# A hybrid encoder layer on one core: weights rounded earlier, weight sums pipelined, and work tied behind other work

## The chip, the core and the metric

The kernel runs on one core of a Trainium2 chip. Its engines run side by side and synchronise through semaphores: PE multiplies matrices, DVE works elementwise with two inputs, ACT evaluates functions, copies and casts, POOL does slow elementwise work, and SP only issues DMAs. The metric is the device time of one execution in microseconds (us), and the median of several runs is compared. The text calls on-chip memory SBUF, the accumulator banks PSUM, and the DRAM behind the chip DRAM.

## The reference

One layer on x of 1024 tokens by 1024 features, everything in float32:

```python
h = rmsnorm(x, g1)
p = h @ w_in                               # gb, gc, gv | q, k, v, go | two low-rank gates
y_a = gb * dwconv3(gc * gv)                # short convolution over tokens, 512 columns
y_b = silu(go) * headnorm(gla(q, k, v) + flipped gla)   # 4 heads of gated linear attention
x = x + rmsnorm(concat(y_a, y_b) @ w_out, gpost)
h = rmsnorm(x, g2)
u = dwconv3(h @ w_up)                      # 5632 columns: 2816 gate, 2816 value
x = x + rmsnorm((silu(u_gate) * u_value) @ w_down, gpost2)
```

## The kernel before

Every float32 product is made of three PE passes. An operand is split by `split` (L671) into a rounded high part (an ACT cast) and a rest (a DVE subtraction); high times high, high times low and low times high are added in PSUM. So nearly every PE operand needs one ACT and one DVE instruction after its DMA has landed.

**Mixer.** Per-token norms and transposes give hT; the value columns come first (tile `pv`, L328). The small low-rank gate values `lr` (L336 to L338) are transposed by PE as `plr` (L397). `swish_gate` (L598) makes one tile of silu(go) for each of four heads (PE tile `pgo`). Attention (`gla_head`, L451) then alternates with the convolution columns (`conv_tile`, L604): states S, outputs `po`, their norm `on` (L585, L589), the transposes `pot` (L595), and the convolution's `u`. Attention's work tiles have tags of their own (qd, kd, m, cum, kin, koT, sq, cc, cu, S).

**Output projection.** `w_out` is loaded in eight row tiles (wo4 to wo7, then wo0 to wo3) through a ring of three raw tiles and split into `woh` and `wol` (L676 to L684). The y tiles are split into yh and yl (L687), and `w_out_tile` (L699) multiplies them (tile `pw`, L709).

**Up stage.** The up product and the down product use a Strassen-type scheme of seven products on 2x2 blocks (Winograd's form), so sums of weight blocks are needed beside the weights. POOL makes them in units: `up_begin` and `up_end` (24 units wu0 to wu23), `down_begin` and `down_end` (11 units wd0/1 to wd20/21). A unit loads two tiles, does four elementwise operations and stores the result to DRAM. `side` (L135) runs the next unit. It is called eight times in the mixer; in the up stage `up` (L937) calls it with a tiny ACT copy `pace` (L959), which each of a unit's loads waits for; the remainder runs at L1078. `up(c)` runs over 22 column tiles c; its PSUM banks pa, pb, pc are added by DVE into `cv` and `cg` (L956, L975, L978, L986, L989). `gate_and_store` (L1000) convolves both (uv, uu), applies SiLU (L1006) and multiplies (L1008); products and their sums go to DRAM as `actd`.

**Down stage.** Seven products in the order 2, 1, 3, 6, 5, 7, 4 over eleven pairs q. `operands` (L1037) loads an activation half (`actd`) and a weight half (w_down or the stored sums `wdd`), and splits them; `big_product` (L1066) multiplies (tiles pda to pdd, L1063). `evict` (L1081) takes banks out with ACT or DVE. At the end each row tile is squared, scaled (yg, L1128 and L1134), added to the saved x2 (`x2r`, L1113) and stored (L1123); rows 0 to 3 are complete before the last product, rows 4 to 7 finish with it.

**What sets the order.** The program is written in Python order, and a scheduler places each engine's instructions; an engine executes its own list strictly in order. `keep` pins instructions, tile rings bound how early a load can start, and all DMAs but POOL's are issued by SP in order.

Of the kernel before, what the change touches and what calls it, by code (L numbers as in the profile page):

```python
# [40 lines left out]
def kernel(
# [50 lines left out]
    def up_begin(i, tile, after):  # L92
# [163 lines left out]
    lrT = gp.tile([96, L], F32R, tag="lrT", name="lrT")  # L256

# [3 lines left out]
    with ExitStack() as n1:  # L261
# [111 lines left out]
        for t in range(1, NT):  # L373
# [12 lines left out]
            if t >= 2:  # L386
                side(after=hs[t][:, 0:1])
# [52 lines left out]
    mp = mix.enter_context(tc.tile_pool(name="mp", bufs=1))  # L440
# [4 lines left out]
    yT = [None] * KT  # L445
# [3 lines left out]
    nc.vector.memset(S[DK:P, NC - 1, :], 0.0)  # L449

    def gla_head(h):  # L451
# [46 lines left out]
        A = mp.tile([P, HALF], F32, tag="A", name=f"A{h}")  # L498
# [21 lines left out]
        def states(i):  # L520
# [14 lines left out]
            for par in range(2):  # L535
# [6 lines left out]
                nc.scalar.copy(S[DK:P, c0 - 1 : c0 - 1 + 2 * n - 1 : 2, :], kvv[DK:P, par, i0:4, :])  # L542
# [122 lines left out]
    act2 = ffn.enter_context(tc.tile_pool(name="act2", bufs=3))  # L665
# [27 lines left out]
    cvp = ffn.enter_context(tc.tile_pool(name="cvp", bufs=3))  # L693
# [87 lines left out]

    n_raw = [0]
# [216 lines left out]

    def gate_and_store(c, cg, cv):  # L1000
# [21 lines left out]
        nc.sync.dma_start(out=act_d[q][:, 3:5, :], in_=z12)  # L1022
        nc.sync.dma_start(out=act_d[q][:, 5:7, :], in_=z34)
# [13 lines left out]
    def operands(m, q, tile=None):  # L1037
# [3 lines left out]
        nc.sync.dma_start(out=raw[:, 0, :], in_=act_d[q][:, w[0], :])  # L1041
# [13 lines left out]
        split(h, l, raw)  # L1055
# [22 lines left out]
    while jobs:  # L1078
        side()
    y += [row_tile(f"y{t}") for t in range(4, NT)]  # L1080
    def evict(rows, half, bank, add=None):  # L1081
        for t in range(4):
# [3 lines left out]
            else:  # L1086
                nc.vector.tensor_add(o, y[add[0] + t][:, add[1]], bank[t])
# [98 lines left out]
```

## Time and profile before

| | us |
|---|---|
| median of three runs | 1088.48 (1084.95 to 1091.08) |
| the profiled execution's own time | 1082.93 |
| its span, first to last instruction | 1081.2 |
| PE busy | 1056.0 |
| DVE, ACT, POOL busy | 794.9, 466.2, 343.4 |

The granted clock is 0.997 of full speed over the span. A matmul row's duration overlaps the next one's, so a stretch's pace is read from the starts. A timeline row gives the start, the duration, the engine, the line, the operation and tiles; a bracket gives the idle time just before it and what ended that idle time.

### The profile page before, as it was taken

The numbers are of one execution on the slowest core, as the hardware profiler recorded it, in microseconds if no ns is written. First come the engines' busy times: TensorE is split into PE (matmuls) and PEld (weight loads), VectorE is DVE, ScalarE is ACT, GpSimd is POOL, SyncE is SP. The second block draws the span as 40 slices with busy tenths as digits, with TensorE's granted clock in tenths as the row PEclk, the third lists the DMA queues.
The fourth block names the chain that finished last, engine by engine and source line by source line (L and its number), as shares of the span: only waits on it lengthen the run. The fifth ranks groups of instructions, "written<-read, shape, count | busy, mean of one in ns | idle before, by whom it ended". The sixth has DMA issues, their size and how long they took to land.

```text
span 1081.2 us, 14384 instructions
## 1 busy us (share of the span) xinstructions
PE 1056.0 (98%) x5409; PEld 871.2 (81%) x5409; DVE 794.9 (74%) x990; ACT 466.2 (43%) x654; POOL 343.4 (32%) x358
## 2 busy tenths in 40 slices
PE   8999999999999999999999999999999999999997
PEld 7988887788887888777888888888888788878876
DVE  6641369879837657989987987987798867645685
ACT  6422354453326335544444434344444435334651
POOL 2785200000000000045465554547456455440000
PEclk9999999999999999999999999999999999999999
DMA  8776211110106423168877867775877789977783
GB/s 281 270 257 208 85 40 37 41 40 21 39 21 233 156 79 108 60 189 271 290 230 259 275 230 243 252 261 153 256 254 273 281 290 322 329 274 229 263 261 152
DMA packets 163800, 211.17 MB, mean 195 GB/s; under 512 B 18305, under 2 KB 113682, under 8 KB 163730
## 3 DMA queue, kind: packets, MB, share of 16 engines
q1 hardware_dynamic: 144594, 141.04, 40.6%
q0 software_dynamic: 19136, 69.21, 18.3%
q8 instruction: 42, 0.69, 0.3%
q14 instruction: 28, 0.23, 0.1%
HBM read 147.04 MB, written 63.18 MB: 194 GB/s over the span
## 4 chain that ended last, share of the span: by engine, by line
PE 33%; DMA 20%; POOL 20%; issue 12%; DVE 11%; ACT 3%; SPq 0%; DVEq 0%; POOLq 0%; ACTq 0%
PE pw L709 7%; PE pgc L223 4%; PE pgo L223 4%; PE pv L328 4%; PE pgv L223 3%; PE pqk L223 3%; PE pgb L223 2%; PE pdb L1063 2%; DVE d L673 2%; DVE t L673 1%; DMA wd15r<-in_w_down_dram 1%; DMA d_7r<-wdd 1%; DMA wd20r<-in_w_down_dram 1%; DMA wd17r<-in_w_down_dram 1%; DVE yl L673 1%
## 5 line engine op out<-in xcount | busy, mean ns | idle before, releaser
L1063 PE MATMUL pdb<-d 128*128 128x512 f32 (+1 forms) x495 | 110.7, 384 | 2.5 <-ACT y L1108 1.2
L99 POOL COPY wu8g<-pace 128x1 f32<-128x1 f32 x1 | 0.5, 532 | 353.5 <-ACT pace L959 353.5
L1063 PEld LDWEIGHTS pdb<-d 128*128 128x128 f32 x495 | 90.6, 188 | 22.3 <-ACT y L1108 1.6
L779 PE MATMUL pb<-t,uv 128*128 128x512 f32 x264 | 64.6, 394 | 0.1
L779 PEld LDWEIGHTS pb<-t,uv 128*128 128x128 f32 x264 | 49.3, 188 | 12.1 <-DVE cv L978 0.6
L1006 ACT ACTIVATE uu<-uu 128x1024 f32<-128x1024 f32 x22 | 23.4, 1062 | 44.0 <-DVE uu L933 44.0
L709 PE MATMUL pw<-woh,yh 128*128 128x512 f32 x128 | 39.7, 395 | 1.9 <-ACT woh L672 1.9
L709 PE MATMUL pw<-wol,yh 128*128 128x512 f32 x128 | 40.1, 393 | 0.3 <-DVE wol L673 0.3
L709 PE MATMUL pw<-woh,yl 128*128 128x512 f32 x128 | 39.8, 390 | 0.0
L956 DVE TENSOR_TENSOR cg<-cv,pb 128x512 f32<-128x512 f32 x22 | 15.1, 685 | 32.1 <-PE pb L779 15.0
L1008 DVE TENSOR_TENSOR uu<-uu,uv 128x1024 f32<-128x1024 f32 x22 | 30.2, 1374 | 3.0 <-ACT uu L1006 2.9
L932 DVE SCALAR_TENSOR_TENSOR uu<-cg,prm,uu 128x1023 f32<-128x1023 f32 x22 | 30.7, 1393 | 1.9
L1063 PE MATMUL pdc<-d 128*128 128x512 f32 x132 | 30.2, 390 | 0.0
L1063 PE MATMUL pdd<-d 128*128 128x512 f32 x132 | 30.2, 390 | 0.0
L933 DVE SCALAR_TENSOR_TENSOR uu<-cg,prm,uu 128x1023 f32<-128x1023 f32 x22 | 30.2, 1372 | 0.0
L932 DVE SCALAR_TENSOR_TENSOR uv<-cv,prm,uv 128x1023 f32<-128x1023 f32 x22 | 29.7, 1351 | 0.0
L709 PEld LDWEIGHTS pw<-woh,yh 128*128 128x128 f32 x128 | 23.7, 188 | 7.3 <-ACT woh L672 2.6
L933 DVE SCALAR_TENSOR_TENSOR uv<-cv,prm,uv 128x1023 f32<-128x1023 f32 x22 | 29.1, 1322 | 0.0
L1063 PEld LDWEIGHTS pdd<-d 128*128 128x128 f32 x132 | 24.8, 188 | 5.3
L1063 PEld LDWEIGHTS pdc<-d 128*128 128x128 f32 x132 | 24.8, 188 | 5.3
L709 PEld LDWEIGHTS pw<-wol,yh 128*128 128x128 f32 x128 | 24.0, 188 | 5.9 <-DVE wol L673 0.7
L709 PEld LDWEIGHTS pw<-woh,yl 128*128 128x128 f32 x128 | 24.0, 188 | 5.4
(1276 smaller groups left out, 3151.6 us busy)
## 6 DMA issues: line engine op xcount, KB each, us to landing
actd<-as SPq DMA_DIRECT2D x22, 512.0 KB, 5.7
x<-in_x_dram SPq DMA_DIRECT2D x16, 512.0 KB, 4.0
actd<-uu SPq DMA_DIRECT2D x11, 512.0 KB, 4.8
x2d<-x SPq DMA_DIRECT2D x8, 512.0 KB, 2.9
x2r<-x2d SPq DMA_DIRECT2D x8, 512.0 KB, 6.1
out_dram<-o SPq DMA_DIRECT2D x7, 512.0 KB, 2.6
actd<-uu SPq DMA_DIRECT2D x11, 256.0 KB, 4.2
d_0r<-actd SPq DMA_DIRECT2D x7, 256.0 KB, 5.3
```

What stands on the lines that cost most here:

```text
L99: nc.gpsimd.tensor_copy(w[:, 0, 0:1], after)
L223: nc.tensor.matmul(o[hf], wt[:, k, :], act[hf][a][:, k, :], start=(k == 0 and wt is wh and a == 0), stop=(k == KT - 1 and wt is wl))
L328: keep(nc.tensor.matmul(ps[:, n * 512 : n * 512 + VH], a[:, k, sl], w[:, k % 2, n * VH : (n + 1) * VH], start=(j == 0), stop=(j == 3 * KT ...
L673: nc.vector.tensor_sub(lo, src, hi.bitcast(F32))
L709: ins = nc.tensor.matmul(ps[:, n * HALF : (n + 1) * HALF], a[:, k, sl], w[:, n * HALF : (n + 1) * HALF], start=(i == 0 and q == 0), stop=( ...
L779: nc.tensor.matmul(o, w[:, k, :], m[:, k, :], start=start and k == 0 and q == 0, stop=k == 3 and q == 2, skip_group_check=True)
L932: nc.vector.scalar_tensor_tensor(u[:, 1:L], src[:, 0 : L - 1], ffn_tap(0, r), u[:, 1:L], op0=ALU.mult, op1=ALU.add)
L933: nc.vector.scalar_tensor_tensor(u[:, 0 : L - 1], src[:, 1:L], ffn_tap(2, r), u[:, 0 : L - 1], op0=ALU.mult, op1=ALU.add)
L956: nc.vector.tensor_add(cg[:, hi], cv[:, lo], pb)
L1006: nc.scalar.activation(ug, ug, AF.Silu)
L1008: nc.vector.tensor_mul(ug, ug, uv)
L1063: nc.tensor.matmul(o, a[:, 0, sl], b[:, 1, r], start=start and i == 0, stop=stop and i == 2, skip_group_check=True)
```

## The change

Eight things change; which numbers are computed does not.

1. `swish_gate(0)` is written ahead of the transposes pprm and plr.
2. Units are pipelined in the mixer: the next unit's load is issued before the last one's operations. Ten units begin there (eight before), 25 are left (27 before).
3. The split of w_out goes into attention's work tiles as they come free (`homes`), and is tied behind the last S copy on ACT. Attention's pool lives until the up stage begins.
4. At c = 0 the addition of `cg` (L956) gets high priority.
5. Pacing starts at c = 3 (c = 1 before), with double units at 8, 11, 14.
6. Product 2's splits from q = 4 on are tied behind the SiLU of c = 20.
7. The last pair's stores are issued by ACT, and products 2 and 1 take that pair's activations from SBUF. Some of the last POOL units get spare weight tiles.
8. At the end the squares and scalings of rows 0 to 3 are tied behind the last evictions, and these rows' x2r loads and stores are issued by POOL.

```diff
+PACE_0 = 3
...
-    def side(tile=row_tile, after=None):
+    begun, loads = [], []
+    def side(tile=row_tile, after=None, ahead=0):
         if jobs:
             begin, end, i = jobs.pop(0)
-            end(i, *begin(i, tile, after))
+            begun.append((end, i, begin(i, tile, after)))
+        while len(begun) > ahead:
+            end, i, t = begun.pop(0)
+            with tc.issue_after(loads[-1].ins) if ahead else ExitStack():
+                end(i, *t)
...
             if t >= 2:
-                side(after=hs[t][:, 0:1])
+                side(after=hs[t][:, 0:1], ahead=1)
+        swish_gate(0)
+        side(ahead=1)
         pp = ps_tile("pprm")
...
-    mp = mix.enter_context(tc.tile_pool(name="mp", bufs=1))
+    units = ExitStack()
+    mp = units.enter_context(tc.tile_pool(name="mp", bufs=1, side="right"))
...
-                nc.scalar.copy(S[DK:P, c0 - 1 : c0 - 1 + 2 * n - 1 : 2, :], kvv[DK:P, par, i0:4, :])
+                last_act[0] = nc.scalar.copy(S[DK:P, c0 - 1 : c0 - 1 + 2 * n - 1 : 2, :], kvv[DK:P, par, i0:4, :])
...
-    for h in range(HEADS):
+    for h in range(1, HEADS):
         swish_gate(h)
-        if h < 2:
-            side()
+        side(ahead=h < HEADS - 1)
...
+    homes = [("qd", "kd"), ("m", "cum"), ("kin", "koT"), ("qd", "r"), ("r", "r"), ("S",), ("w", "sq"), ("cc", "cu")]
...
-        split(*wo[k], raw)
+        with tc.issue_after(last_act[0].ins):
+            split(*wo[k], raw)
...
-        nc.vector.tensor_add(cg[:, hi], cv[:, lo], pb)
-        if c >= 1:
+        with tc.high_priority() if c == 0 else ExitStack():
+            nc.vector.tensor_add(cg[:, hi], cv[:, lo], pb)
+        if c >= PACE_0:
...
-            for _ in range(2 if c in (2, 5, 8, 11) else 1):
+            for _ in range(2 if c in (8, 11, 14) else 1):
                 side(late_tile, pace)
...
+        act_after[c] = last_act[0]
...
+        store = (nc.scalar if q == NQ - 1 else nc.sync).dma_start
...
+        here = m < 3 and q == NQ - 1
+        if not here:
+            nc.sync.dma_start(out=raw[:, 0, :], in_=act_d[q][:, w[0], :])
...
-        split(h, l, raw)
+        with tc.issue_after(act_after[NFC - 2].ins) if m == 2 and q >= 4 else ExitStack():
+            if here:
+                split(h[:, 1], l[:, 1], raw[:, 1])
+                split(h[:, 0], l[:, 0], last[m][:, 0:HALF])
+            else:
+                split(h, l, raw)
...
     while jobs:
-        side()
+        side(late_tile if len(jobs) % 3 == 0 else spare_tile)
...
-        nc.sync.dma_start(out=x2, in_=x2d[t])
+        (nc.gpsimd if t < 4 else nc.sync).dma_start(out=x2, in_=x2d[t])
...
-        nc.scalar.activation(o, y[t], AF.Square, accum_out=ss[:, 0:1])
-        nc.vector.tensor_mul(yg, y[t], gpost2)
-        finish(t, x2, yg, o, rstd_of(ss[:, 0:1], D))
+        with tc.issue_after(done_a.ins), tc.issue_after(done_v.ins):
+            nc.scalar.activation(o, y[t], AF.Square, accum_out=ss[:, 0:1])
+            nc.vector.tensor_mul(yg, y[t], gpost2)
+            finish(t, x2, yg, o, rstd_of(ss[:, 0:1], D))
```

Three places of the new order follow. The first is ACT's list at the tail of attention; gb3 is the last convolution weight, c, on, rs and u belong to the last convolution tile and the last head, and wo4 to wo7, wo0, wo1 are rows of w_out (wo_2940 is the high part of wo1, in the place of S). Before:

```order
L542 COPY S<-kv_1_2533 64x4x128
L181 CAST gb3h<-gb3r 128x1024
L608 COPY c_2702<-pgc_2653 128x1024
L585 ACTIVATE on_2737<-po_2704 128x1024
L160 ACTIVATE rs<-ssh_2739,eps 128x8
L162 ACTIVATE rs<-rs 128x8
L614 ACTIVATE u_2808<-c_2702,prm 128x1024
L672 CAST yh_2928<-yT_1001 128x512
L672 CAST yh_2928<-yT_1068 128x512
L672 CAST yh_2928<-yT_1135 128x512
L672 CAST yh_2928<-yT_1192 128x512
...
L672 CAST woh_2889<-wo4r 128x1024
```

Now:

```order
L565 COPY S<-kv_1_2553 64x4x128
L687 CAST wo4h<-wo4r 128x1024
L687 CAST wo5h<-wo5r 128x1024
L190 CAST gb3h<-gb3r 128x1024
L687 CAST wo6h<-wo6r 128x1024
L625 COPY c_2722<-pgc_2673 128x1024
L608 ACTIVATE on_2757<-po_2724 128x1024
L687 CAST wo7h<-wo7r 128x1024
L687 CAST wo_2940<-wo1r 128x1024
L169 ACTIVATE rs<-ssh_2759,eps 128x8
L687 CAST wo0h<-wo0r 128x1024
L171 ACTIVATE rs<-rs 128x8
```

The casts of w_out moved from behind yh to places between the last head's instructions, six of them ahead of rs's second half and u.

The second place is ACT's list at the end of the up stage; uu are the gate tiles of c = 20 and 21, L1006 (L1041 now) is SiLU, d are operands of the down stage's product 2. Before:

```order
L959 COPY pace_7004<-cg_7002 128x1
L931 ACTIVATE uu_7048<-cg_6858,prm 128x1024
L672 CAST d_6_7261<-d_6r 128x1024
L967 COPY cg_7002<-pa_6974 128x512
L672 CAST d_4_7226<-d_4r 128x1024
L1006 ACTIVATE uu_7048<-uu_7048 128x1024
L672 CAST d_2h<-d_2r 128x1024
```

Now:

```order
L961 ACTIVATE uu_7036<-cg_6846,prm 128x1024
L999 COPY cg_6990<-pa_6962 128x512
L687 CAST d_0h<-d_0r 128x1024
L1041 ACTIVATE uu_7036<-uu_7036 128x1024
L687 CAST d_1h<-d_1r 128x1024
L687 CAST d_4_7224<-d_4r 128x1024
L687 CAST d_4_7224<-d_5r 128x1024
L1050 DMA actd_3958<-uu_7036 128x512
L687 CAST d_6_7259<-d_6r 128x1024
L961 ACTIVATE uv_7083<-cv_6963,prm 128x1024
L687 CAST d_2h<-d_2r 128x1024
```

The copy of cg and SiLU moved ahead of the casts of d_4 and d_6, and the last pair's store now stands in ACT's list.

The third place is DVE's list near the end; d are operands of the last product, y the output rows, L1087 (L1134 now) an eviction, L1122 the final addition of rows 0 and 1. Before:

```order
L673 TENSOR_TENSOR d_6_8383<-d_6r,d_6_8383 128x1024
L673 TENSOR_TENSOR d_6_8383<-d_7r,d_6_8383 128x1024
L1122 SCALAR_TENSOR_TENSOR o_8410<-yg_8411,rs,x2r_8408 128x1024
L1122 SCALAR_TENSOR_TENSOR o_8428<-yg_8429,rs,x2r_8426 128x1024
L673 TENSOR_TENSOR d_8_8394<-d_8r,d_8_8394 128x1024
L673 TENSOR_TENSOR d_8_8394<-d_9r,d_8_8394 128x1024
L673 TENSOR_TENSOR d_10_8405<-d_10r,d_10_8405 128x1024
L1087 TENSOR_TENSOR y_7141<-y_7141,pdb_7350 128x512
L1087 TENSOR_TENSOR y_7142<-y_7142,pdb_7351 128x512
L1087 TENSOR_TENSOR y_7143<-y_7143,pdb_7350 128x512
L1087 TENSOR_TENSOR y_7144<-y_7144,pdb_7351 128x512
L1122 SCALAR_TENSOR_TENSOR o_8446<-yg_8447,rs,x2r_8444 128x1024
```

Now:

```order
L688 TENSOR_TENSOR d_8_8394<-d_8r,d_8_8394 128x1024
L688 TENSOR_TENSOR d_8_8394<-d_9r,d_8_8394 128x1024
L688 TENSOR_TENSOR d_10_8405<-d_10r,d_10_8405 128x1024
L1134 TENSOR_TENSOR y_7139<-y_7139,pdb_7349 128x512
L1134 TENSOR_TENSOR y_7140<-y_7140,pdb_7350 128x512
L1134 TENSOR_TENSOR y_7141<-y_7141,pdb_7349 128x512
L1134 TENSOR_TENSOR y_7142<-y_7142,pdb_7350 128x512
L1177 TENSOR_TENSOR yg_8429<-y_7106,gpost_7103 128x1024
L1177 TENSOR_TENSOR yg_8411<-y_7105,gpost_7103 128x1024
L170 TENSOR_SCALAR rv<-ssf_8412,eps 128x1
L1184 TENSOR_TENSOR yg_8483<-y_7139,gpost_7103 128x512
```

The evictions now follow the splits directly, and the scaling yg of rows 0 to 3 comes behind them.

## Rows read from the trace of the kernel before

**Rows 1.** the page: busy us, share of the span and instructions by engine
```profile
PE 1056.0 (98%) x5409; PEld 871.2 (81%) x5409; DVE 794.9 (74%) x990; ACT 466.2 (43%) x654; POOL 343.4 (32%) x358
```

**Rows 2.** PE's waits: line, tile waited with, releaser: us in total, times, longest
```profile
PE pc L779 <- DVE cv L975: 2.7, 2, 2.1
PE plr L397 <- DVE lr L338: 2.4, 1, 2.4
PE pw L709 <- ACT woh L672: 1.9, 1, 1.9
...
PE pb L779 <- DVE cg L956: 1.7, 1, 1.7
...
PE pdb L1063 <- ACT y L1108: 1.2, 1, 1.2
PE pdb L1063 <- DVE d L673: 0.8, 1, 0.8
...
PE pdb L1063 <- ACT d L672: 0.5, 1, 0.5
```

**Rows 3.** two windows: PE, PEld, DVE, ACT, POOL busy, PEclk, DMA share, GB/s
```profile
837.00:864.00 27.00, 24.91 (x102) 19.83 (x101) 23.60 (x23) 13.79 (x16) 13.45 (x16) 0.94 0.79 280
1053.00:1080.00 27.00, 21.18 (x124) 18.49 (x122) 16.32 (x38) 4.96 (x18) 0.00 (x0) 0.95 0.43 168
```

**Rows 4.** timeline of DVE, 64 to 72: start, duration, engine, line, [idle before]
```profile
65.27 2.31 DVE L182 TENSOR_TENSOR go1l<-go1r,go1h 128x1024 fp32r<-128x1024 f32 x1
...
70.15 0.82 DVE L338 CAST lr<-lr 128x32 fp32r<-128x32 f32 x1
```

**Rows 5.** timeline of ACT, 300 to 331
```profile
302.53 1.01 ACT L608 COPY c<-pgc 128x1024 f32<-128x1024 f32 x1 [10.32 <-PE pgc L223]
...
317.78 1.16 ACT L614 ACTIVATE u<-c,prm 128x1024 f32<-128x1024 f32 x1 [9.50 <-DVE c L612]
...
329.13 1.04 ACT L672 CAST woh<-wo4r 128x1024 fp32r<-128x1024 f32 x1
```

**Rows 6.** DMA issues in 290 to 330: KB each, median us to landing
```profile
wo6r<-in_w_out_dram SPq DMA_DIRECT2D x1, 512.0 KB, 3.5
```

**Rows 7.** timeline of DVE, 450 to 457
```profile
455.30 0.68 DVE L956 TENSOR_TENSOR cg<-cv,pb 128x512 f32<-128x512 f32 x1
```

**Rows 8.** timeline of DVE, 474 to 494
```profile
477.51 2.21 DVE L1008 TENSOR_TENSOR uu<-uu,uv 128x1024 f32<-128x1024 f32 x1
...
492.42 1.23 DVE L1008 TENSOR_TENSOR uu<-uu,uv 128x1024 f32<-128x1024 f32 x1
```

**Rows 9.** timeline of ACT, 838 to 856
```profile
848.62 1.05 ACT L672 CAST d<-d_6r 128x1024 fp32r<-128x1024 f32 x1 [4.88 <-DMA d_6r<-in_w_down_dram]
```

**Rows 10.** timeline of DVE, 844 to 862
```profile
852.09 2.07 DVE L1008 TENSOR_TENSOR uu<-uu,uv 128x1024 f32<-128x1024 f32 x1 [2.91 <-ACT uu L1006]
...
860.32 0.68 DVE L986 TENSOR_TENSOR cg<-cg,pc 128x512 f32<-128x512 f32 x1
```

**Rows 11.** timeline of PE, 857 to 870
```profile
867.57 0.39 PE L1063 MATMUL pda<-d_3h 128*128 128x512 f32 x1
```

**Rows 12.** timeline of ACT, 495 to 500
```profile
497.82 0.19 ACT L959 COPY pace<-cg 128x1 f32<-128x1 f32 x1 [1.25 <-DVE cg L956]
```

**Rows 13.** timeline of POOL, 505 to 520
```profile
512.05 0.64 POOL L99 COPY wu10g<-pace 128x1 f32<-128x1 f32 x1 [0.55 <-DMA wud<-wu9v]
```

**Rows 14.** timeline of POOL, 950 to 962
```profile
956.01 0.56 POOL L128 DMA_DIRECT2D wdd<-wd19r  x1
```

**Rows 15.** timeline of ACT, 945 to 972
```profile
965.90 1.05 ACT L672 CAST d<-d_6r 128x1024 fp32r<-128x1024 f32 x1 [13.53 <-DMA d_6r<-wdd]
```

**Rows 16.** timeline of SP's queue, 1030 to 1042
```profile
1036.44 2.53 SPq L1113 DMA_DIRECT2D x2r<-x2d  x2
```

**Rows 17.** timeline of DVE, 1040 to 1081
```profile
1047.92 2.47 DVE L1087 TENSOR_TENSOR y<-y,pdb 128x512 f32<-128x512 f32 x4
...
1074.22 0.42 DVE L1148 TENSOR_TENSOR y<-y,pdl 128x256 f32<-128x256 f32 x1 [2.86 <-PE pdl L1063]
```

More of the change, by code (lines that the diff above doesn't have):

```diff
@@ L99, in up_begin @@
                 nc.gpsimd.tensor_copy(w[:, 0, 0:1], after)
-            nc.gpsimd.dma_start(out=w, in_=w_up[:, k::4, c + g * HALF : c + g * HALF + n])
+            load = nc.gpsimd.dma_start(out=w, in_=w_up[:, k::4, c + g * HALF : c + g * HALF + n])
+        loads.append(load)
         return t
@@ L256, with swish_gate @@
     lrT = gp.tile([96, L], F32R, tag="lrT", name="lrT")
+    yT = [None] * KT
+    def swish_gate(h):
+        w = load_cols([(w_in, O_GO + h * P, P)], f"go{h}")
+        ps = feature_chunk(w, hT, f"pgo{h}")
+        yT[4 + h] = ypool.tile([P, L], F32, tag="y", name=f"yT{4 + h}")
+        nc.scalar.activation(yT[4 + h], ps, AF.Silu)
     NPB = 21
@@ L497, in gla_head @@
         nc.scalar.copy(koT, pk)
-        A = mp.tile([P, HALF], F32, tag="A", name=f"A{h}")
+        A = gp.tile([P, HALF], F32, tag="A", name=f"A{h}")
         tiles = {}
@@ L863 @@
     ep.close()
+    units.close()
+    act2 = ffn.enter_context(tc.tile_pool(name="act2", bufs=3, side="right"))
     sp = ffn.enter_context(tc.tile_pool(name="sp", bufs=N_R))
@@ L998, in up @@
         return gate_and_store(c, cg, cv)
+    act_after = {}
+    last = {}
     def gate_and_store(c, cg, cv):
@@ L1009, in gate_and_store @@
         q = c // 2
+        store = (nc.scalar if q == NQ - 1 else nc.sync).dma_start
         if c % 2 == 0:
             odd[q] = ug
-            nc.sync.dma_start(out=act_d[q][:, 0, :], in_=ug[:, lo])
+            store(out=act_d[q][:, 0, :], in_=ug[:, lo])
             return
         a1, a2 = odd[q], ug
-        nc.sync.dma_start(out=act_d[q][:, 1:3, :].rearrange("p a t -> p (a t)"), in_=a2)
+        store(out=act_d[q][:, 1:3, :].rearrange("p a t -> p (a t)"), in_=a2)
+        last[1], last[2] = a1, a2
         z12, z34 = (row_tile(f"as{q}{x}").rearrange("p (a t) -> p a t", a=2) for x in ("12", "34"))
@@ L1021, in gate_and_store @@
         nc.vector.tensor_sub(z34[:, 1], a2[:, lo], z12[:, 1])
-        nc.sync.dma_start(out=act_d[q][:, 3:5, :], in_=z12)
-        nc.sync.dma_start(out=act_d[q][:, 5:7, :], in_=z34)
+        store(out=act_d[q][:, 3:5, :], in_=z12)
+        store(out=act_d[q][:, 5:7, :], in_=z34)
     rest = iter(())
@@ L1035, with operands @@
     n_op = [0]
-    def operands(m, q, tile=None):
+    def operands(m, q):
         raw = raw_tile([P, 2, HALF], f"d{m}_{q}r")
         w = which[m]
-        nc.sync.dma_start(out=raw[:, 0, :], in_=act_d[q][:, w[0], :])
+        here = m < 3 and q == NQ - 1
+        if not here:
+            nc.sync.dma_start(out=raw[:, 0, :], in_=act_d[q][:, w[0], :])
         if w[1] is None:
@@ L1086, in evict @@
             else:
-                nc.vector.tensor_add(o, y[add[0] + t][:, add[1]], bank[t])
+                done = nc.vector.tensor_add(o, y[add[0] + t][:, add[1]], bank[t])
+        return done if add else None
     pa = four_banks("pda")
@@ L1104 @@
     big_product(7, pb, False)
-    evict(4, hi, pb, (4, hi))
+    done_v = evict(4, hi, pb, (4, hi))
     nc.scalar.copy(y[4][:, lo], pb[0])
-    nc.scalar.copy(y[NT - 1][:, 256:HALF], pb[3][:, 256:HALF])
+    done_a = nc.scalar.copy(y[NT - 1][:, 256:HALF], pb[3][:, 256:HALF])
     ops4 = [operands(4, q) for q in range(NQ)]
```

34 lines of the change are left out of this document (18 added, 16 removed).

## The prediction

> **What bounds the kernel now.** I read the head of the page first [rows 1]: PE is busy 1056.0 us, 98% of the span, so PE bounds the kernel, and since the change leaves PE's multiplications as they are, it can only win PE's idle time (some 25 us) and what the clock loses after a pause. Next comes the view of PE's waits [rows 2], which names each gap's size and the last releaser. Seven kinds of gap bear on this change: 2.4 us at `plr`, 1.9 at the first `pw` on a cast of w_out, 1.7 at `pb` on the sum cg, 2.7 at `pc` on cv (one of 2.1, so the other is 0.6), and 1.2, 0.8 and 0.5 in the down stage. Last, for each gap, comes the timeline of the engine that releases it, to see whether it was slow, queued behind other work, or waited for a DMA. That decides whether moving an instruction helps.
>
> **The gaps, one by one.**
>
> *plr, 2.4 us.* The last `lr` copy runs at 70.15 because DVE took the splits of go1 and go2 first, 2.31 us each [rows 4], before PE could transpose. With swish_gate(0) in front, PE has 48 full-size products between the value columns and `plr`; the go0 split that they need was made ahead of those two. A row of that size lasts 0.39 us [rows 11] and overlaps the next; even at half of it the 48 last over 9 us, and from 65.27 to the end of the last copy are under 6. Gain 2.4; bounds 1 and 2.4.
>
> *pw, 1.9 us.* The cast of wo4 stands behind yh and runs at 329.13, while ACT had idled 10.32 us up to 302.53 and 9.50 up to 317.78 [rows 5]. The tile's data are not late; the place in the list is. The change puts six of the eight casts ahead of rs's second half and u. Six casts of 1.04 are 6.2 us, which either idle stretch covers if the raw tiles have landed. A load takes 3.5 us from issue to landing [rows 6] and the ring holds three, so a tile needs about (3.5 + 1.04 + 1.2)/3 = 1.9 us, eight need 15, and from the start of the first idle stretch, 292.2, to u there are 25.6. Gain 1.9; bounds +1.9 and, if u slips by the two casts in front of it, 1.9 - 2.1 = -0.2. I take 1.9, since the nearest row is that idle time.
>
> *pb, 1.7 us.* cg's addition at 455.30 has no idle time in front of it [rows 7]: it stood queued behind subtractions of the T blocks. High priority puts it ahead of them. Those subtractions then come 0.68 us later, for products that come later still. Gain 1.7, bounds 1.0 and 1.7.
>
> *pc early in the up stage, 0.6 us.* DVE's L1008 takes 2.21 us beside POOL's sums and 1.23 without POOL [rows 8]. With pacing from c = 3 POOL is silent here. Gain 0.6. The Trainium skill (GPSIMD Engine Reference, 8. Key points) says that GpSimd shares its SBUF interfaces with VectorE and contends with instructions of two SBUF inputs; the trace agrees, 2.21 against 1.23.
>
> *pc at the last column tile, 2.1 us and the clock.* ACT idled 4.88 us for the DMA of d_6r until 848.62 [rows 9], with SiLU of c = 20 queued behind that cast. So DVE waited 2.91 us for SiLU, multiplied until 854 [rows 10], and only then made the cv that PE needed. The granted clock in 837 to 864 is 0.94 [rows 3]: at half clock for t us, half of t is lost, so (1 - 0.94) x 27 = 1.6 us more are gone. Tying the splits of q >= 4 behind SiLU takes that DMA out of the way. Gain 2.1 + 1.6 = 3.7. New here: the splits of q = 2 and 3 now stand behind the multiplications. PE takes d_3 at 867.57 [rows 11], 3.7 earlier now, at 863.9. DVE adds cg at 860.32 [rows 10], 3.7 earlier 856.6, and from there has 0.68, three convolution steps of about 1.3, and the splits d_2l and d_3l of about 1.2: 856.6 + 7.0 = 863.6, just in time. Where POOL works beside it, each can cost up to 1 us more (2.21 less 1.23). So a new wait of 0 to 4 us; I take 0.5, as only one or two of POOL's four operations fall there.
>
> *The down stage, 0.8 + 0.5.* SP's list stood at a load of `wdd` whose weight sums were not stored: POOL issued wd19r's store at 956.01 [rows 14], ACT idled 13.53 us until 965.90 [rows 15]. Now the paced units begin at c = 3, at 497.82 [rows 12], with the eleventh unit, which before began at 512.05 [rows 13]. From there each unit waits for the one before it, so the chain ends at least 14.2 us earlier, and more where spare tiles let loads run beside. PE arrives earlier by the terms above, 2.4 + 1.9 + 1.7 + 0.6 + 3.7 = 10.3. The chain wins. The last pair no longer makes its way through DRAM before products 2 and 1, and no PE gap stood there. Gain 1.3, bounds -3 and 1.3.
>
> *The last evictions, 1.2.* They begin at 1047.92 [rows 17] with no idle time in front, behind rows 0 to 3 and behind d_8 to d_10, for which SP's list stood 2.53 us at x2r loads [rows 16]. Now they follow the splits directly. Gain 1.2. By the Trainium skill (DMA: Bandwidth & Descriptors, Issuing engines are not separate DMA queues) moving these loads to POOL saves only issue time, since all DMAs share 16 engines; the row shows that here the issue itself stood still for 2.53 us. By the rule alone this term would be near zero and the forecast 1 us higher. The price: four scalings (1.2), four final additions (1.3) and small operations (0.7), some 13 us of DVE, now run behind the evictions. DVE is busy 16.32 of the 27 us from 1053 [rows 3]; the 10.7 idle us hold most of it, but some 3 of them wait for PE's last bank until 1074.22 [rows 17]. Bounds of the price 0 and 4, I take 0.5.
>
> *At no cost:* two more units in the mixer, and the stores on ACT. POOL's operations are the same in number; the two lie beside the gates' products, where DVE has little.
>
> **Sum.** 2.4 + 1.9 + 1.7 + 0.6 + 3.7 + 1.3 + 1.2 = 12.8, less 0.5 and 0.5: 11.8. The profiled execution took 1082.93, span and 1.7 around it; with the change 1071.1. The median of the runs is 5.6 above the profiled one. Taken from the median, 1088.5 - 11.8 = 1076.7.
>
> **Rivals.**
>
> A. *POOL's chain sets the end.* If spare tiles come late and POOL, with DVE beside it denser now, runs each unit longer, so that wd19 is stored at 956 as before, PE arrives 10.3 earlier and waits them all: what is left is 12.8 - 10.3 - 1.3 = 1.2 and the time 1087. For it: SP stood at exactly this store. Against: two fewer units and 14.2 us of lead.
>
> B. *The freed gaps become the next waits.* The splits of d_2 and d_3 late by 3, the tail by 3, and half of `pw` lost: 12.8 - 7 = 6, time 1082.5. For it: 863.6 against 863.9. Against: POOL has gaps for its DMAs in every unit.
>
> C. *Slower, attention's tail.* The casts of w_out stand in ACT's strict list ahead of rs and u. If a raw tile took x us to land, eight tiles through a ring of three take 8 (x + 2.2)/3; in the 25.6 us up to u that holds up to x = 7.4, and from x = 12.2 the wait exceeds all gains. At x = 14 PE waits 43.2 - 25.6 = 17.6, time 1088.5 - 12.8 + 17.6 = 1093. Against it: 3.5 in this stretch [rows 6].
>
> D. *The change doesn't do what it says.* The releasers in the view of waits are those that came last; with others just behind them, each gap shrinks by a third at most: 4 us, time 1084.5.
>
> **Chances.** Forecast 0.62, B 0.15, A 0.08, D 0.08, C 0.07. What a measurement here can tell from no change is 0.5%, 5.4 us; faster means below 1083.0. The forecast gives nearly all of its share to faster, B about half, A and D almost none, and the runs of before spread over 6 us: faster 0.70, same 0.22, slower 0.08. The likeliest case alone reaches from 1071 (all gaps gone, nothing new, and the profiled run's level in part) to 1081. With B, D and A partly inside, the range is 1069 to 1087.
>
> **What would show it.** In the profile after: PE goes through pgo's first 48 matmuls without a pause, and `plr`, `pw` on a cast of w_out and `pb` on cg vanish from PE's waits or stay under 0.3 us; PEclk is 1.00 around the last column tile; ACT no longer waits there for a DMA ahead of SiLU; SP issues the loads of d_9 in product 3 without standing for `wdd`; evictions follow the last splits within 1 us. Wrong would be: PE waiting for d_2l or d_3l by more than 1 us (the step on product 2), a wait at `pot` or at `pw` on yh (attention's tail), ACT idle over 10 us for `wdd` (the chain), or more than 8 us from PE's last matmul to the end of the span, about 7 now.

## The result and the profile after

| | before | changed |
|---|---|---|
| median, us | 1087.91 (1084.95 to 1091.08, 6 runs) | 1075.18 (1074.22 to 1081.14, 6 runs) |
| ratio, with its 95% interval | | 0.989 (0.9862 to 0.9917) |
| the profiled execution, its span | 1082.93, 1081.2 | 1075.13, 1073.2 |

The kernel became 1.1% faster; 1076.7 had been predicted, with a range of 1069 to 1087. But the two profiled executions differ by only 8 us and the medians by 12.7. Before's profiled run (1082.93) lies below all of its timed runs, so its gaps need not be those of a usual run. A second trace of before, in the first experiment, shows what was gained.

The head of the page after, answering to [rows 1]: PE's busy time has grown by 1.0 us, though it issues the same 5409 instructions.

```profile
PE 1057.0 (98%) x5409; PEld 871.0 (81%) x5409; DVE 801.8 (75%) x992; ACT 466.0 (43%) x654; POOL 345.2 (32%) x360
```

PE's waits after, answering to [rows 2] (line, tile, releaser: us in total, times, longest):

```profile
PE pot L618 <- DVE on L612: 1.8, 1, 1.8
...
PE pda L1110 <- DVE d_2l L688: 0.9, 1, 0.9
PE pda L1110 <- DVE d_3l L688: 0.8, 1, 0.8
...
PE pdb L1110 <- DVE d L688: 0.3, 1, 0.3
```

`plr`, `pw` on a cast, `pb` on cg, `pc` on cv and the three `pdb` gaps of before are gone; the `pdb` line that is left stands elsewhere, in product 1 at the last pair. New are the waits for d_2l and d_3l in product 2. (`pot` stood there before.) The windows, answering to [rows 3], first around `pw`, then the last column tile, then the last evictions:

```profile
324.00:351.00 27.00, 27.00 (x118) 21.87 (x117) 19.16 (x34) 13.36 (x26) 0.00 (x0) 1.00 0.47 151
...
837.00:864.00 27.00, 25.25 (x107) 19.56 (x107) 25.14 (x21) 12.54 (x14) 14.47 (x13) 1.00 0.77 267
...
1026.00:1053.00 27.00, 27.00 (x120) 22.07 (x119) 20.51 (x39) 12.38 (x31) 3.39 (x7) 1.00 0.63 206
```

The granted clock around the last column tile is 1.00, before 0.94, and the last evictions no longer cost PE anything. DVE after shows why d_2l is late, and how the tail runs (timeline: start, duration, work, idle before):

```profile
844.94 2.32 DVE L1044 TENSOR_TENSOR uu<-uu,uv 128x1024 f32<-128x1024 f32 x1
...
847.79 1.72 DVE L688 TENSOR_TENSOR d<-d_4r,d 128x1024 fp32r<-128x1024 f32 x1
849.43 2.31 DVE L688 TENSOR_TENSOR d<-d_5r,d 128x1024 fp32r<-128x1024 f32 x1
...
852.26 1.21 DVE L688 TENSOR_TENSOR d_1l<-d_1r,d_1h 128x1024 fp32r<-128x1024 f32 x1
853.40 1.21 DVE L688 TENSOR_TENSOR d<-d_6r,d 128x1024 fp32r<-128x1024 f32 x1
...
856.33 1.21 DVE L688 TENSOR_TENSOR d_2l<-d_2r,d_2h 128x1024 fp32r<-128x1024 f32 x1
...
1036.36 1.22 DVE L688 TENSOR_TENSOR d<-d_10r,d 128x1024 fp32r<-128x1024 f32 x1
1037.49 2.47 DVE L1134 TENSOR_TENSOR y<-y,pdb 128x512 f32<-128x512 f32 x4
...
1066.02 0.42 DVE L1198 TENSOR_TENSOR y<-y,pdl 128x256 f32<-128x256 f32 x1 [0.90 <-PE pdl L1110]
```

The splits of d_4, d_5 and d_6, which PE needs only later, stand in DVE's list ahead of d_2l; POOL's sums (841.96 to 850.66) make the first three operations shown last 1.72 to 2.32 us. d_3l is late for another reason: ACT waits until 859.40 for the load of d_3r. The Trainium skill (GPSIMD Engine Reference, 8. Key points) says GpSimd contends with VectorE's instructions of two SBUF inputs; the trace agrees, 2.31 us beside POOL's sums and 1.21 for the same shape after them. In the tail the evictions follow the last split directly, as predicted, and DVE waits 0.90 us for the last bank (2.86 in [rows 17]). From PE's last row to the end of the span it is 7.2 us, before 7.1: the work moved there fitted in.

### The profile page after: what moved, and what is told of

Same layout as the page of the kernel before. It is cut to its first block, busy times and chain, and to the rows that moved or that the text cites. A ratio compares the mean times of both kernels' runs of the same rounds, so it can differ in the third digit from the quotient of the medians.

```text
span 1073.2 us, 14378 instructions
## 1 busy us (share of the span) xinstructions
PE 1057.0 (98%) x5409; PEld 871.0 (81%) x5409; DVE 801.8 (75%) x992; ACT 466.0 (43%) x654; POOL 345.2 (32%) x360
## 4 chain that ended last, share of the span: by engine, by line
PE 83%; DVE 8%; DMA 3%; ACT 2%; issue 2%; SPq 0%; DVEq 0%; ACTq 0%
PE pb L804 17%; PE pc L804 11%; PE pa L804 9%; PE pw L734 8%; PE pdb L1110 8%; PE pgc L232 4%; PE pgo L232 4%; PE pv L345 4%; PE pgv L232 3%; PE pqk L232 3%; PE pdd L1110 3%; PE pdc L1110 3%; PE pgb L232 2%; DVE d L688 1%; PE pdl L1110 1%
## 5 line engine op out<-in xcount | busy, mean ns | idle before, releaser
L1041 ACT ACTIVATE uu<-uu 128x1024 f32<-128x1024 f32 x22 | 23.4, 1062 | 35.2 <-DVE uu L963 35.1
L1044 DVE TENSOR_TENSOR uu<-uu,uv 128x1024 f32<-128x1024 f32 x22 | 32.4, 1475 | 0.0
L962 DVE SCALAR_TENSOR_TENSOR uu<-cg,prm,uu 128x1023 f32<-128x1023 f32 x22 | 29.0, 1316 | 1.9
L873 ACT COPY cv<-pa 128x512 f32<-128x512 f32 x22 | 12.8, 587 | 38.1 <-PE pa L804 36.1
L963 DVE SCALAR_TENSOR_TENSOR uu<-cg,prm,uu 128x1023 f32<-128x1023 f32 x22 | 29.3, 1333 | 0.0
L570 DVE SCALAR_TENSOR_TENSOR S<-S,dec 64x128 f32<-64x128 f32 x56 | 19.2, 344 | 10.7 <-ACT S L561 8.5
L961 ACT ACTIVATE uv<-cv,prm 128x1024 f32<-128x1024 f32 x22 | 25.4, 1154 | 3.7 <-DVE cv L1021 3.5
L961 ACT ACTIVATE uu<-cg,prm 128x1024 f32<-128x1024 f32 x22 | 25.3, 1149 | 0.3 <-ACT d L687 0.3
L1018 DVE TENSOR_TENSOR cg<-cg,pc 128x512 f32<-128x512 f32 x22 | 15.0, 680 | 8.9 <-PE pc L804 8.9
```

What stands on the lines that cost most here:

```text
L570: nc.vector.scalar_tensor_tensor(S[0:DK, c + 1, :], S[0:DK, c, :], dec[0:DK, c : c + 1], S[0:DK, c + 1, :], op0=ALU.mult, op1=ALU.add)
L961: nc.scalar.activation(u, src, AF.Copy, scale=ffn_tap(1, r))
L962: nc.vector.scalar_tensor_tensor(u[:, 1:L], src[:, 0 : L - 1], ffn_tap(0, r), u[:, 1:L], op0=ALU.mult, op1=ALU.add)
L963: nc.vector.scalar_tensor_tensor(u[:, 0 : L - 1], src[:, 1:L], ffn_tap(2, r), u[:, 0 : L - 1], op0=ALU.mult, op1=ALU.add)
L1041: last_act[0] = nc.scalar.activation(ug, ug, AF.Silu)
```

## The experiments

Each was timed beside before on its own chip; ratios are to that before.

**c_before: the kernel before, unchanged, once more.**

> The kernel before once more, with a profile. The profiled pair differs by 8.0 us in span (1081.2 and 1073.2), the medians by 12.7 (1087.91 and 1075.18), and the profiled run of before was the fastest of its runs. Theory: the gaps of before vary from run to run, above all those that end with a DMA (the splits ahead of SiLU at the last column tile, SP's hold at wdd), so this trace shows the same seven gaps, some of them longer, and a run near 1087. Rival: the gaps are the same and matmuls follow each other more slowly in most runs (231 to 232 ns a matmul in the up stage instead of 230).

Measured: 1090.38 (1087.95 to 1092.71, 12 runs) against 1089.39, ratio 1.0008 (0.9989 to 1.0027), profiled span 1086.6. PE's waits:

```profile
PE plr L397 <- DVE lr L338: 3.2, 1, 3.2
PE pc L779 <- DVE cv L975: 2.6, 2, 2.1
PE pda L1063 <- ACT d L672: 2.3, 1, 2.3
PE pw L709 <- ACT woh L672: 1.9, 1, 1.9
...
PE pb L779 <- DVE cg L956: 1.6, 1, 1.6
PE pda L1063 <- DVE d L673: 1.6, 1, 1.6
```

PE behind `plr`, and at the end of product 2:

```profile
71.93 0.32 PE L397 MATMUL plr<-ident,lr 128*96 128x128 f32 x1 [3.22 <-DVE lr L338]
...
72.31 1.04 PE L223 MATMUL pgo<-hTh,go0h 128*128 128x512 f32 x2
...
75.71 0.65 PE L223 MATMUL pgo<-hTl,go0h 128*128 128x512 f32 x2
...
891.33 0.65 PE L1063 MATMUL pda<-d 128*128 128x512 f32 x1 [2.34 <-ACT d L672]
893.61 4.97 PE L1063 MATMUL pda<-d 128*128 128x512 f32 x11 [1.63 <-DVE d L673]
```

ACT at that end:

```profile
890.23 1.04 ACT L672 CAST d<-d_10r 128x1024 fp32r<-128x1024 f32 x1 [15.54 <-DMA d_10r<-actd]
```

and the window around it (PE busy, PEld, DVE, ACT, POOL, PEclk, DMA share, GB/s):

```profile
880.00:907.00 27.00, 23.03 (x90) 18.16 (x89) 12.84 (x9) 10.75 (x13) 11.04 (x14) 0.87 0.89 311
```

What follows: this run of before loses at two places that its first profile hardly showed, and at 1088.29 it lies among the usual ones. Behind `plr` the pair of rows takes 1.04 us until 75.7, then 0.65: the 3.2 us gap is followed by some 3.4 us at the lower clock level, which cost 1.7 more. At the end of product 2, the operand d_10, the last pair, comes back from DRAM late; ACT waits 15.54 us, PE 2.3 and 1.6, and the clock falls to 0.87 in the window. The first trace was close to the same gap; ACT there:

```profile
884.80 1.05 ACT L672 CAST d<-d_10r 128x1024 fp32r<-128x1024 f32 x1 [12.20 <-DMA d_10r<-actd]
```

DVE's split of d_10 ended there at 887.11, and PE took that part at 887.16: nothing was to spare. On the other hand the gaps at the `wdd` hold and the last evictions are absent in this trace. PE's starts in after are earlier than here by 5.1 us at the first `pg`, 7.2 at the first `pw`, 6.5 at the first `pa`, 10.5 at product 2's start, 14.9 at product 1's, 13.5 at the last product's; the span is 13.4 shorter, which fits the medians.

**c_after: the changed kernel once more.**

> The changed kernel once more. Its first trace has matmuls of the output projection starting 232 ns apart (229 before) and those of the up stage 231 to 233 (230 before). Theory: that belongs to this kernel, and this trace shows 232 again. Rival: it belongs to the run, and the distances differ from the first trace by 1 ns or more. Time 1074 to 1076 by both.

Measured: 1077.58 (1074.81 to 1078.86, 5 runs), ratio 0.9898 (0.988 to 0.9916), span 1075.4. The `pdb` line, 0.3 in the first trace and there at the last pair, is now a wait at d_4:

```profile
PE pdb L1110 <- DVE d L688: 2.2, 1, 2.2
```

DVE ahead of it:

```profile
890.07 2.31 DVE L688 TENSOR_TENSOR d<-d_5r,d 128x1024 fp32r<-128x1024 f32 x1
892.30 2.32 DVE L688 TENSOR_TENSOR d<-d_6r,d 128x1024 fp32r<-128x1024 f32 x1
894.55 0.68 DVE L688 TENSOR_TENSOR d<-uu,d 128x512 fp32r<-128x512 f32 x1
895.15 1.21 DVE L688 TENSOR_TENSOR d<-d_4r,d 128x1024 fp32r<-128x1024 f32 x1
```

What follows: in product 1 DVE takes d_5 and d_6 ahead of d_4, which PE needs first, 2.3 us each beside POOL's sums, which run until 893.5 (1.21 each in the first trace, where these sums end at 889.7). This wait depends on the run: 0 to 2.7 us in the later kernels. A second finding is no gap at all: PE's rows start 232.1 ns apart in the output projection, in both traces of after, and 229.0 in both of before (means of the distances of successive starts of full-size rows).

**x_notie: the changed kernel without part 6's tie.**

```diff
-        with tc.issue_after(act_after[NFC - 2].ins) if m == 2 and q >= 4 else ExitStack():
+        with ExitStack():
```

> The changed kernel without the tie of product 2's splits (q from 4 on) behind the SiLU of column tile 20. In its lists only one line moves: ACT casts d_4 ahead of that SiLU. Theory (the tie took away the 2.1 us gap and the half clock): the gap returns in part, pc waits for cv for 0.5 to 2 us, time 0.5 to 3.7 us more than the changed kernel. Rival: the pacing and the order of loads had already moved the late cast, and the tie is worth nothing: no wait at pc, time within 0.5 us, and the waits for d_2l and d_3l stay at 0.7 to 0.9 us each.

Measured: 1076.26 (1073.58 to 1078.2, 5 runs), ratio 0.9888 (0.987 to 0.9905). One line of ACT's list moves, and PE does not wait at `pc`; d_2l waits 0.9 and d_3l 0.5, as with the tie. The tie is worth nothing that can be measured; which other part moved SiLU ahead of the late cast is not shown.

**x_dram: the changed kernel with the last pair's operands from DRAM, stored by SP.** Of part 7 only POOL's spare tiles stay.

```diff
-        store = (nc.scalar if q == NQ - 1 else nc.sync).dma_start
+        store = nc.sync.dma_start
...
-        here = m < 3 and q == NQ - 1
+        here = False
```

> The changed kernel with its seventh part undone: the last pair's products are stored by SP and products 2 and 1 load them back from DRAM. Theory: in most runs before, PE waited for this round trip at the end of product 2 (2.3 and 1.6 us and half clock behind it in the repeat's trace), and the prediction's zero for this part was wrong: PE waits 2 to 6 us for d of product 2's last pair and the time is 3 to 7 us more than the changed kernel. Rival: in the changed kernel the other parts have made room for it; no wait over 0.5 us there, time within 1 us.

Measured: 1082.93 (1081.43 to 1087.25, 7 runs), ratio 0.9958 (0.9941 to 0.9974). Its waits, and ACT:

```profile
PE pda L1110 <- ACT d L687: 3.7, 1, 3.7
PE pdb L1110 <- DVE d L688: 2.3, 1, 2.3
...
PE pda L1110 <- DVE d L688: 1.5, 1, 1.5
```

```profile
883.33 1.04 ACT L687 CAST d<-d_10r 128x1024 fp32r<-128x1024 f32 x1 [13.04 <-DMA d_10r<-actd]
```

The gap of c_before is back at the same operand. So this half of part 7 is worth 5.4 to 7.8 us (1082.93 less the two medians of the changed kernel), the largest gain of a part that was tried alone.

**x_tail: the changed kernel without part 8.**

```diff
-        (nc.gpsimd if t < 4 else nc.sync).dma_start(out=x2, in_=x2d[t])
+        nc.sync.dma_start(out=x2, in_=x2d[t])
...
-            (nc.gpsimd if t < 4 else nc.sync).dma_start(out=out[t * P : (t + 1) * P, r], in_=o[:, r])
+            nc.sync.dma_start(out=out[t * P : (t + 1) * P, r], in_=o[:, r])
...
-        with tc.issue_after(done_a.ins), tc.issue_after(done_v.ins):
+        if True:
...
-        with tc.issue_after(done_a.ins):
+        if True:
```

The last hunk is a tie of the squares of rows 4 to 7, which the change has too.

> The changed kernel with its eighth part undone: squares, scalings, x2r loads and stores of rows 0 to 3 as before, all on SP's queue and untied. Theory: the part was worth what its gap cost, pdb waits again for the last evictions, 0 to 2.2 us and half clock behind it: 0 to 3 us more, 1.2 in the mean. Rival (its price in DVE work behind the evictions eats it): within 0.5 us or faster.

Measured: 1075.57 (1074.75 to 1079.92, 5 runs), ratio 0.9891 (0.9874 to 0.9909); the gap at the evictions is back with half its size, and the median lies between the two of the changed kernel (1075.18 and 1077.58):

```profile
PE pdb L1110 <- ACT y L1156: 0.6, 1, 0.6
```

The other `pdb` waits of this trace, 0.2 and 0.8, stand at the first row of product 6: ACT waited 12.56 us for d_0r, a load of the stored sums, and PE lost 0.9 by it.

**x_p14: the kernel before with parts 1 and 4 alone** (eight mixer units as before).

```diff
+        swish_gate(0)
+        side()
...
-    for h in range(HEADS):
+    for h in range(1, HEADS):
...
-        nc.vector.tensor_add(cg[:, hi], cv[:, lo], pb)
+        with tc.high_priority() if c == 0 else ExitStack():
+            nc.vector.tensor_add(cg[:, hi], cv[:, lo], pb)
```

> The kernel before with parts 1 and 4 alone: swish_gate(0) ahead of pprm and plr, and high priority for the sum cg of c = 0. Theory (the prediction's terms add up): the gaps at plr (2.4 in the first trace, 3.2 and half clock in the repeat's) and at pb (1.7) go and nothing comes in their place: 4 to 6 us less than before. Rival (the time is given back later, since the gaps behind are DMA-bound and only grow): less than 2 us gained, with longer waits in product 2 or at wdd.

Measured: 1085.62 (1082.41 to 1091.26, 12 runs), ratio 0.9978 (0.9961 to 0.9995): 2.4 us. `plr` and `pb` are gone, worth 5.1 and 1.6 in c_before, but `pc` has grown from 2.6:

```profile
PE pc L781 <- DVE cv L978: 6.3, 4, 3.1
```

DVE ahead of the longest one:

```profile
494.94 2.31 DVE L934 SCALAR_TENSOR_TENSOR uv<-cv,prm,uv 128x1023 f32<-128x1023 f32 x1
497.17 2.31 DVE L934 SCALAR_TENSOR_TENSOR uu<-cg,prm,uu 128x1023 f32<-128x1023 f32 x1
...
501.61 0.67 DVE L978 TENSOR_TENSOR cv<-cv,pc 128x512 f32<-128x512 f32 x1
```

Here POOL's sums (493.07 to 500.60) lie beside the convolutions that PE waits for, and part of the freed time is given back there; `pda` and `pdb` wait for splits too, 3.0 in all. With parts 1 and 4 done, pacing from c = 3 is worth up to 5.1 us, by this argument (the two waits at the early column tiles, 2.0 and 3.1), not 0.6.

**x_pace1: the changed kernel with before's pacing** (one double unit fewer, since two more units lie in the mixer).

```diff
-PACE_0 = 3
+PACE_0 = 1
...
-            for _ in range(2 if c in (8, 11, 14) else 1):
+            for _ in range(2 if c in (2, 5, 8) else 1):
```

> The changed kernel with pacing from c = 1 and double units at 2, 5 and 8 (part 5 undone, ten units still in the mixer). Theory: POOL's sums lie again beside DVE's convolutions of the early column tiles, pc waits 0.5 to 0.8 us at c = 2 as before; the chain ends earlier, and since it no longer bounds anything nothing is gained for it: 0.5 to 1 us more than the changed kernel. Rival: the earlier end takes POOL's last sums away from the splits of product 1, whose DVE waits (0.3 to 2.7 us, run by run) go: the same or up to 2 us less.

Measured: 1119.27 (1116.87 to 1127.04, 6 runs), ratio 1.0297 (1.0267 to 1.0327).

```profile
PE pda L1110 <- ACT d_3h L687: 36.5, 1, 36.5
PE pc L804 <- DVE cv L1007: 6.4, 4, 3.5
```

```profile
904.39 1.04 ACT L687 CAST d_3h<-d_3r 128x1024 fp32r<-128x1024 f32 x1 [42.68 <-DMA wdd<-wd20r]
```

POOL's unit that d_3h stands behind:

```profile
880.22 0.53 POOL L120 DMA_DIRECT2D wd20r<-in_w_down_dram  x1
...
901.35 0.57 POOL L130 DMA_DIRECT2D wdd<-wd20r  x1
```

No theory foresaw it. The 6.4 us at `pc` are the price of early pacing. The 36.5 come from a side effect: one unit is left at the end of the up stage where the changed kernel leaves three, and it takes spare tiles from the ring of weight tiles from which d_3h, the high part of d_3, gets its place. The load of d_3r was issued at 858; it is the cast that waits, until the unit is stored, and POOL stores it only behind the sums of the next unit. So the run bears out the price at `pc` and says nothing on pacing as a whole.

**x_place: the kernel before, the operand tiles act2 on the other side of SBUF.** In the changed kernel they lie there. In before they hold the parts of w_out, then the T blocks; the tiles allocated behind them move as well. The instruction lists are those of before.

```diff
-    act2 = ffn.enter_context(tc.tile_pool(name="act2", bufs=3))
+    act2 = ffn.enter_context(tc.tile_pool(name="act2", bufs=3, side="right"))
```

> The kernel before with nothing changed but the SBUF addresses of the pool act2 (and so of those behind it), as in the changed kernel; every engine's list of instructions is the same. Theory: the addresses of the tiles that PE streams set the distance of matmuls: 232 ns in the output projection and 231 to 233 in the products on T blocks, so 3 to 4 us more than before. Rival: the addresses do nothing; distances as in the repeat of before, time within 1 us of it.

Measured: 1091.86 (1087.27 to 1097.23, 12 runs), ratio 1.0034 (1.0017 to 1.0052); rows 232.8 ns apart in the output projection (229.0 in c_before). By the ratio the places cost 3.7 us, by the medians 2.5; the rows' distances alone, over the 384 rows of the output projection and 1320 on T blocks, make 4.1. A window without any gap, in the output projection, shows it in the count of rows (PE busy, its rows in brackets, PEclk, DMA share, GB/s); first c_before, then after, then x_place:

```profile
350.00:380.00 30.00, 30.00 (x133) 1.00 0.53 176
```

```profile
350.00:380.00 30.00, 30.00 (x131) 1.00 0.30 105
```

```profile
350.00:380.00 30.00, 30.00 (x130) 1.00 0.52 176
```

The trace of x_place is also a third one of before's lists, and it has two gaps that c_before lacks, at the `wdd` hold (0.8) and at the last evictions (2.1); the one at d_10 is there again (2.0):

```profile
PE pdb L1063 <- ACT y L1108: 2.1, 1, 2.1
PE pda L1063 <- ACT d L672: 2.0, 1, 2.0
```

**x_align, x_prio, x_left, x_low12: the changed kernel with its tiles elsewhere.** x_align puts an unused tile of 32 bytes at the top of the right side, x_prio adds high priority for the first splits of product 2, x_left has this priority without the pad and moves act2 back to the left side, and x_low12 is x_prio with a pad of 1184 bytes, so that the addresses agree with before's in their low 12 bits.

```diff
+    padp = ctx.enter_context(tc.tile_pool(name="padp", bufs=1, side="right"))
+    padp.tile([P, 8], F32, tag="pad", name="pad")      # x_align, x_prio
+    padp.tile([P, 296], F32, tag="pad", name="pad")    # x_low12
...
-        with tc.issue_after(act_after[NFC - 2].ins) if m == 2 and q >= 4 else ExitStack():
+        with tc.high_priority() if m == 2 and q < 4 else tc.issue_after(act_after[NFC - 2].ins) if m == 2 else ExitStack():    # x_prio, x_left, x_low12
...
-    act2 = ffn.enter_context(tc.tile_pool(name="act2", bufs=3, side="right"))
+    act2 = ffn.enter_context(tc.tile_pool(name="act2", bufs=3))                 # x_left
```

> The changed kernel with an unused tile of 32 bytes per partition at the top of the right side of SBUF, so that attention's tiles, the w_out pieces and act2 begin at multiples of 64 bytes (180160) and not 32 above one (180192). All lists of instructions stay as they are. Theory (32 bytes off slow PE's streaming): starts of matmuls 229 ns apart in the output projection (232 now) and 230 in the products on T blocks (231.4 to 233.6 now), so 3 to 4 us less than the changed kernel, 1072 to 1074. Rival (the place in SBUF counts, left or right, not the 32 bytes): 232 and 233 stay and the time is within 1 us of the changed kernel.

> As x_align, and product 2's splits of q below 4 are given high priority: DVE subtracts d_1l ahead of cv and d_2l ahead of the last convolution. Theory: PE's waits for d_2l and d_3l (0.3 to 0.9 us each) come from DVE's order, and go: 0.5 to 1.5 us less than x_align. Rival: d_3r's load ends them (it is issued only when the tile of d_1r is free); d_2l's wait goes, d_3l's stays, less than 0.7 us gained.

> As x_prio, but act2 opens on the left side at 170816 instead of on the right at 180160; the lists differ only where the T blocks are first built (430 to 455 us). 170816 equals the place of before, 142144, in its low 12 bits; attention's tiles and the w_out pieces stay on the right, 32 bytes off. Theory (the low address bits of a streamed tile set its pace): matmuls on T blocks start 230 ns apart again, as before, against 231.2 to 232.7 in x_align; 1 to 1.5 us less than x_prio. Rival (the region counts): 231 to 233 stay and the time is within 1 us of x_prio. The output projection keeps 232 by both.

> As x_prio with the unused tile at the top of the right side 1184 bytes instead of 32 per partition; all lists are the same. Attention's tiles, the w_out pieces and act2 then begin at 179008, which equals the 142144 of before in its low 12 bits; the region is the one of x_prio. Theory (the low address bits of a streamed tile set its pace): starts of matmuls 229 ns apart in the output projection (231.2 in x_prio) and 230 in the products on T blocks (231.2 to 232.7); 1.5 to 2.5 us less than x_prio, 1071.5 to 1072.5. Rival (some other property of the left side): 231 and 232 stay, time within 1 us of x_prio's 1074.0.

| kernel | act2 at, its low 12 bits | rows apart, ns: output projection; up stage, T blocks | median, us | ratio |
|---|---|---|---|---|
| before | 142144, 2880 | 229.0; 230.1 | | |
| changed | 180192, 4064 | 232.1; 231.3 to 233.6 | 1075.18 | 0.989 (0.9862 to 0.9917) |
| x_align | 180160, 4032 | 231.2; 231.2 to 232.7 | 1074.46 | 0.9878 (0.9861 to 0.9895) |
| x_prio | 180160, 4032 | as x_align | 1074.02 | 0.9862 (0.9844 to 0.9879) |
| x_left | 170816, 2880 | 232.1; 229.9 to 230.5 | 1075.14 | 0.9885 (0.9862 to 0.9907) |
| x_low12 | 179008, 2880 | 228.9; 229.8 to 230.5 | 1073.55 | 0.9849 (0.9807 to 0.9891) |

In the changed kernels the parts of w_out lie mostly in attention's tiles, which begin where act2 does later, in x_left on the right at 4064 as in the changed kernel. The rows of x_low12 in the window:

```profile
350.00:380.00 30.00, 30.00 (x133) 1.00 0.30 105
```

Before's pace is back with before's low address bits, though the tiles lie 36,864 bytes away from before's: the low bits set the pace, not the side. An alignment to 64 bytes (x_align) gives back about a quarter. The Trainium skill (SBUF — State Buffer, Operand start alignment) lets a float32 operand start at any multiple of 4 bytes and adds that its runs timed nothing; all the places here are such, and the time of a row differs by 1.4%. x_left, with act2 alone moved, has the old pace on the T blocks only (the w_out tiles stayed), but builds them later, and PE waits for them:

```profile
455.29 3.01 PE L805 MATMUL pb<-t,uv 128*128 128x512 f32 x12 [1.58 <-DVE cv L1011]
```

x_prio shows what priority does; its waits:

```profile
PE pdb L1113 <- DVE d L691: 2.7, 1, 2.7
...
PE pda L1113 <- DVE d_3l L691: 0.8, 1, 0.8
```

d_2l's wait is gone, d_3l's stays: its raw tile d_3r comes late, since a ring place falls free only with d_1l (split until 852.73, load issued at 852.76). x_low12 has the lowest median of all, 1.6 us below the changed kernel; the intervals overlap, so a faster kernel is not shown by the times, only its pace by the trace.

## Why the prediction was right, and which of its steps were not

The forecast 1076.7 lies 1.5 us from 1075.18, but several of its terms were wrong and balance: that it came so close is in part luck. Sizes are from c_before against after, whose span differs by 13.4.

- *plr, 2.4.* Right in mechanism: the 48 products hide the splits. Mis-sized: 5.1 in a usual run, since the gap is 3.2 there and 1.7 follow at the lower clock, which the first profile did not show.
- *pw, 1.9.* The gap is gone, and ACT casts six tiles ahead of rs's second half, as predicted, and a seventh ahead of u. PE gains 2.6 in this stage (2.1 at the gap, the rest at a late split behind it) and keeps 1.4, since its 384 rows are 3.1 ns further apart each, 1.2 us. Parts 2 and 3 were not tried alone.
- *pb, 1.7.* Right (1.6).
- *pc early, 0.6.* Right for the kernel before, but not as a part of the sum: x_p14 shows that, with `plr` gone, the gaps there without the new pacing would be 5.1.
- *pc at the last column tile, 3.7.* The gap is gone, but the step that credits it to the tie failed: x_notie does without. Nor is it a steady loss: c_before has 2.1 there, x_place, with the same instruction lists, none. The new wait at d_2 and d_3 was foreseen, with bounds of 0 to 4, and mis-sized: 0.5 taken, some 2.5 measured (0.87 at d_2l, 0.12 at d_3h, 0.76 at d_3l, and the slow starts behind them). Of these splits POOL slowed only those of d_4 and d_5, but d_4 to d_6 stand ahead of d_2l on DVE, and that order was not priced, nor that d_3r's load comes late.
- *The down stage, 1.3, and the last evictions, 1.2.* The mechanisms hold: POOL's last sums are stored by 927.4 (956 in [rows 14]), and evictions follow the splits. But the gaps come and go: the three traces of before's lists (before, c_before, x_place) have 1.3, 0 and 0.8 at the hold, and 1.2, 0 and 2.1 at the evictions, where x_place lost 1.5 more at the lower clock (PE's next 99 rows take 20.95 us, 19.42 in the first trace). So the terms are means over runs, near 0.7 and 1.6 in these three. For part 8, x_tail's trace shows 0.6 at the evictions and 0.9 ahead of product 6, its times nothing. The 2.53 us of [rows 16] are two issues together; the loads just ahead of them were issued in 0.32 to 0.44 each, so less than 2.53 was standing still. The price of the tail, 0.5, was 0.2 at most.
- *The last pair through DRAM: "no PE gap stood there", 0.* This is the step that failed most. The gap cost some 6.5 us in c_before, clock included, x_place has 2.8 there and x_p14 2.3, and x_dram brings it back. The profiled run of before just missed it, though ACT stood 12.20 us for d_10r in that run too.
- *The sum taken from the median.* The 5.6 us between that run and the median were taken to stay. They were 2.5 more at `plr` and some 6.5 at product 2, less the gaps that c_before does not have. Counted on c_before by PE's starts, the change won 5.1 at `plr`, and on balance 1.4 in the output projection, 4.1 in the up stage and 4.3 in product 2, and lost 1.4 behind that, 1.1 of it at three short stops in product 1: 13.5, and the spans differ by 13.4. In these balances PE's slower pace took 1.2 and 2.6, and the waits at d_2 and d_3 some 2.5. The prediction had 12.8 less 1.0.

*Rivals.* A is out: in neither trace of the changed kernel does PE wait for POOL's chain (x_tail's has 0.9). B named the right places, d_2 and d_3, but they cost some 2.5, not 3, and the tail nothing. C: the load that ACT waits longest for in attention's tail is wo6, 4.63 us until 294.31, and PE starts `pw` at 325.57. D: part 6 fits it, the whole does not.

*Still open:* why the low bits of an address change PE's pace, which of them, and whether it is the address itself or its distance from PE's other operand, since no run separates the two; what moving the pacing alone is worth, since x_pace1 fell to another wait; and what sets the timing that makes product 1's wait differ from run to run.

## What to carry to other kernels

Take a second trace before pricing gaps: a gap that hangs on a DMA's return, as d_10r here, can be missing from one run and cost 6 us in the next, and a profiled run that is well below the median suggests that something was missing. An engine that stands 12 us for a DMA just ahead of PE is a sign of it, even where PE does not wait. A freed gap is worth what the next stage lets through, so parts are to be priced together (parts 1 and 4 alone gave 2.4 of some 6.7). When tiles move, compare the distance of PE's starts in a stretch without gaps: it is a cost that no view of waits shows.

## What the hardware showed unexpectedly

- PE's pace in rows of 512 columns depends on the low address bits of its operands in SBUF: 229.0 ns from row to row or 232.1, with no gap and a granted clock of 1.00. Over the changed kernel the rows' distances make some 3.8 us of it.
- After a gap of 3.2 us the granted clock stayed at its lower level (1.2 GHz) for about 3.4 us in c_before, while after 2.4 us in the first trace of before the next pair took 0.62 us, without a loss. Yet after the 2.2 us in c_after the rows started 0.43 us apart, from 897.9 to 901.4: the length of the gap alone does not decide it.
- A cast waiting for an operand that was stored to DRAM shortly before it stood 13.04 and 15.54 us.
